# One bank for three running sums: the third product behind the first plain chunk, and a copy by ScalarE in place of an addition

## The chip, the cores and the metric

The kernel runs on 1 core of one Trainium2 chip. The metric is the time of one execution on the device, in microseconds. The engines are called as the profile calls them: PE is TensorE's matmul, PEld its weight load, DVE is VectorE, ACT is ScalarE, POOL is GpSimd, SP is SyncE, which issues the DMAs. `L380` is line 380 of the kernel before.

## The reference, cut to what matters

A decoder trunk of two layers over 256 tokens of width 2048, in float32. Each layer has a mixer (attention and a gated recurrence that share an input and an output projection), a gated FFN, and a small gated embedding, with norms around them. What matters here is that each of these is a set of products `tokens x weights`:

```
proj = h @ w_in                      # 2048 -> all heads
x    = x + norm(mix @ w_out)         # 2048 -> 2048
hid  = silu(h @ w_ffn_gate) * (h @ w_ffn_up)     # 2048 -> 5632, twice
x    = x + norm(hid @ w_ffn_down)    # 5632 -> 2048
g    = gate(x @ w_ple_gate)          # 2048 -> 2048
```

## The kernel before

**Tiles.** The 256 tokens are two blocks of 128 rows. A product is made in columns of 512 (one PSUM bank of 128 x 512 per block), over chunks of 256 rows of the weight matrix. To keep float32's accuracy, weights and activations are each split in a high and a low part. A chunk of weights (tile `wr`, fetched by `fetch_w` L275 on SP) is cast by ACT to its high part `wh` (L281), and DVE subtracts that to get the low part `wl` (L291). One product of a block and a chunk is six matmuls of 128x512: L380 (high x high), L383 (low activations x high weights) and L384 (high activations x low weights), twice each. In the names of the trace, `ck` is a split activation, `sum` (or `nat`) a split sum of activations, `ms` a bank for short use, and `acce`, `acca`, `accc`, `accd` the four accumulators of a pair.

**Pairs.** `paired` works on two columns and both blocks together, 40 times in all (20 for each layer: 2 for w_out, 10 for gate and up, 7 for down, 1 for the embedding's gate). For the first two chunks, `fast` uses a scheme with seven products in place of eight: some products are of sums of tokens (`mix(i)`, made by `mixed`) and of differences of weight chunks (`sub`, L396, in place in the tiles `r11`, `r12`, `r21`, `r22`). The other chunks are plain: `plain` makes one product for each block and chunk.

**The sums in question.** A bank `u` takes the product of block 0 and `r11`; `saved` (L389) has ACT copy it to SBUF as `p1`. Then the product of `mix(2)` is added in the same bank, and ACT copies that as `u2`. A third product, of `mix(3)` and `r12`, has a bank of its own, `u7`. DVE adds `u7` and `u2` to `u3` (L426), and `u3` to `p5` (L427), which is a copy of the first part of `c`. `p1`, `u3`, `u2` and `p5` are added to the accumulators at the end of the pair.

**What sets the order.** The program is written in a plain order, but a scheduler places the instructions on each engine by its own estimates of cost, so the order on an engine is fixed before the run and differs from the text. At run time each engine takes its instructions strictly as they stand, and waits by semaphores. `tick()` lets deferred steps (`later`) in, such as the turning of activations by way of DRAM: `turn<-nat` and `nat<-turn` on SP (L234, L240), with the splits of what comes back by ACT (L179) and DVE (L180). The pools hold 6 tiles `wr`, 7 each of `wh` and `wl`, 12 `nat`, and 4 + 4 PSUM banks (`ms` and `acc`).

Of the kernel before, what the change touches and what calls it, by code (L numbers as in the profile page):

```python
# [12 lines left out]
ALU = mybir.AluOpType  # L13
# [34 lines left out]
def decoder(ctx: ExitStack, tc: tile.TileContext, x, p, positions, w_in, attn_sinks,  # L48
# [16 lines left out]
    V, S, G, T = nc.vector, nc.scalar, nc.gpsimd, nc.tensor  # L65
# [29 lines left out]
    def tick():  # L95
        clock[0] += 1
        for gen in list(running):
            if next(gen, True):
                running.remove(gen)
        for item in [q for q in queue if q[0] <= clock[0]]:  # L100
            queue.remove(item)
            item[1]()

    def nat(shape=(P, W), dt=F32):
        return np_.tile(list(shape), dt, tag="nat", name="nat")

    def bank(shape=(P, W)):
        return pms.tile(list(shape), F32, tag="ms", name="ms")
# [158 lines left out]
    def new_ck():  # L267
        return [xp.tile([P, 4, SEQ], F32R, tag="ck", name="ck", bufs=14) for i in range(2)]
# [4 lines left out]
    def fetch_w(w, c, col):  # L273
        raw = wpr.tile([P, 2, W], F32, tag="wr", name="wr")
        nc.sync.dma_start(raw, w[c * 2 * P:(c + 1) * 2 * P, col:col + W].rearrange(  # L275
            "(k p) n -> p k n", p=P))
        return raw
# [6 lines left out]
    def load_w(w, c, col, raw=None, hi=None):  # L284

        if raw is None:
            raw = fetch_w(w, c, col)
        if hi is None:
            hi = high(raw)
        lo = wps.tile([P, 2, W], F32R, tag="wl", name="wl")  # L290
        marks["lo"] = V.tensor_tensor(lo, raw, hi.bitcast(F32), op=ALU.subtract)  # L291
        return hi, lo
# [68 lines left out]
    def paired(lhs, sums, wa, wb, cols, done_a, done_b, nch=8, row0=0, skews=(0, 0),  # L361
               after=None, mixed_order=False):

        base = row0 // (2 * P)
        opened = {}

        def psum(name):
            return pacc.tile([P, W], F32, tag="acc", name=name)

        def block(c, t):  # L370
            def get(k):
                kt = 2 * c + k
                return tuple(a[:, kt % 4, t * P:(t + 1) * P] for a in lhs[kt // 4])
            return get

        def acc(ps, x, hl):
            hi, lo = hl
            for k in range(2):
                xh, xl = x(k)
                T.matmul(ps, xh, hi[:, k], start=id(ps) not in opened, stop=False,  # L380
                         skip_group_check=True)
                opened[id(ps)] = ps
                T.matmul(ps, xl, hi[:, k], start=False, stop=False, skip_group_check=True)  # L383
                marks["pe"] = T.matmul(ps, xh, lo[:, k], start=False, stop=k == 1,  # L384
                                       skip_group_check=True)

        def saved(ps):
            b = nat()
            S.copy(b, ps)  # L389
            return b  # L390

        def parts(r):
            return load_w(None, 0, 0, raw=r)

        def sub(dst, p, q):
            V.tensor_tensor(dst, p, q, op=ALU.subtract)  # L396

        def fast():
            mix = sums()
            r11, r12 = fetch_w(wa, base, cols[0]), fetch_w(wb, base, cols[1])  # L400
            r21, r22 = fetch_w(wa, base + 1, cols[0]), fetch_w(wb, base + 1, cols[1])
            u = bank()
            acc(u, block(0, 0), parts(r11))
            p1 = saved(u)
            sub(r11, r12, r11)
            c = psum("accc")
            acc(c, mix(1), parts(r11))
            p5 = saved(c)
            tick()
            e = psum("acce")  # L410
            acc(e, block(1, 0), parts(r21))
            sub(r12, r22, r12)
            u7 = bank()
            acc(u7, mix(3), parts(r12))
            tick()
            w22 = parts(r22)
            sub(r22, r22, r11)
            sub(r21, r21, r22)
            acc(u, mix(2), parts(r22))
            u2 = saved(u)  # L420
            a = psum("acca")
            acc(a, block(1, 1), parts(r21))
            tick()
            acc(c, mix(4), w22)
            u3 = nat()
            V.tensor_tensor(u3, u7, u2, op=ALU.add)  # L426
            V.tensor_tensor(p5, u3, p5, op=ALU.add)  # L427
            return e, a, c, (p1, u3), (u2, p5)

        def plain(w, col, banks, skew, end, c0=2, c1=nch):  # L430
            n = c1 - c0
            ws = {}
            for i in range(n + skew):
                if i < n:
                    ws[i] = load_w(w, base + c0 + i, col)
                    acc(banks[0], block(c0 + i, 0), ws[i])
                    if i == n - 1 and end:
                        end(0)
                if i >= skew:
                    acc(banks[1], block(c0 + i - skew, 1), ws[i - skew])  # L440
                tick()
            if end:
                end(1)

        e, a, c, x1, x2 = fast()
        if after:
            after()

        def end_a(t):
            done_a(t, (e, a)[t], x1[t])  # L450

        def end_b(t):
            done_b(t, (c, d)[t], x2[t])
        if mixed_order:
            d = psum("accd")
            plain(wa, cols[0], (e, a), 0, None, c1=nch - 2)
            plain(wb, cols[1], (c, d), 0, None, c1=nch - 2)
            plain(wa, cols[0], (e, a), 0, end_a, c0=nch - 2)
            plain(wb, cols[1], (c, d), 0, end_b, c0=nch - 2)
            return  # L460
        plain(wa, cols[0], (e, a), skews[0], end_a)
        d = psum("accd")
        plain(wb, cols[1], (c, d), skews[1], end_b)

# [203 lines left out]
    for l in range(DEPTH):  # L668
# [4 lines left out]
        mix = {0: attn[0], 1: attn[1]}  # L673
# [450 lines left out]
        for gi, glen in enumerate(FF_GROUPS):  # L1124

            hx = []
            want = ff0 + glen + (glen == 2)
            while len(hidden) < want:
                n = len(hidden)
                gated(n, n == want - 1, hidden[ff0] if n > ff0 else None)  # L1130
            hid = hidden[ff0:ff0 + glen]
            last = gi == len(FF_GROUPS) - 1
            dones = []
            if last:
                nxT = [new_ck() for c in range(4)]
            for s in range(4):
                if gi == 0:
                    macc[s] = sp.tile([P, NT, W], F32, tag="ABCD"[s], name=f"macc{s}")
                if last:
                    gB = load_gain(post_ffn_gain[l], s * W)  # L1140

                def done(t, ps, x, s=s, gB=gB if last else None):
                    m = macc[s][:, t]
                    if gi == 0:
                        V.tensor_tensor(m, ps, x, op=ALU.add)
                        return
                    V.tensor_tensor(m, ps, m, op=ALU.add)
                    if x is not None:
                        V.tensor_tensor(m, x, m, op=ALU.add)
                    if last:  # L1150
                        square_sum(m, ssf[t][:, s:s + 1])
                        V.tensor_tensor(m, m, gB, op=ALU.mult)
                        if s == 3:
                            post_norm(macc, ssf, t, nss, nxT, gain_cols(64, l, 16), (4, 3)[t])
                if last and s == 2:
                    pT2 = sp.tile([P, 2, 2, SEQ], F32R, tag="at", name="pT2")
                    pT = [pT2[:, 0], pT2[:, 1]]
                    for t in range(NT):
                        pn = nat()
                        nc.sync.dma_start(pn[:, 0:256], p[l, 0, t * P:(t + 1) * P, :])  # L1160
                        split_T([pn[:, 0:P], pn[:, P:2 * P]], None, pT, t)
                dones.append(done)
                if last and s >= 2:
                    strip(hid, w_ffn_down[l], s * W, lambda t, ps, done=done: done(t, ps, None),
                          nch=2 * glen, row0=ff0 * W, skew=4 if s == 3 else 0)
                elif s % 2:
                    paired(hid, lambda: hx[0], w_ffn_down[l], w_ffn_down[l], (s * W - W, s * W),
                           dones[s - 1], done, nch=2 * glen, row0=ff0 * W,
                           mixed_order=s == 1)
            ff0 += glen  # L1170
        xT, ss = nxT, nss

# [2 lines left out]
        end = l == DEPTH - 1  # L1175
# [76 lines left out]
```

## Time and profile before

| | us |
|---|---|
| median of 3 runs | 2386.39 |
| lowest, highest | 2385.81, 2387.82 |
| the profiled execution | 2388.4 |
| its span | 2386.7 |

The profiled execution is 2.0 above the median, and 1.7 of its time lies outside its span. Rows of groups read: line, engine, operation, out<-in by names, shapes, count, then busy us, mean ns, and the idle time just before them with what ended it. A matmul of 128x512 is shown with 0.39 us, but the next one starts 0.23 us later: matmuls overlap, and the distance of the starts counts.

### The profile page before, as it was taken

Reading aid. Unit: us, or ns where it says so; the run is one execution under the profiler, and the core shown is the slowest. Engines: PE = TensorE matmul, PEld = TensorE weight load, DVE = VectorE, ACT = ScalarE, POOL = GpSimd, SP = SyncE. Lnnn points to the kernel's source line nnn. Section 1 sums busy time; section 2 is a strip of 40 time slices with the busy share of each in tenths; the row PEclk is TensorE's granted clock in tenths of the full one; section 3 lists DMA queues with packets and bytes.
Section 4 is the critical chain, followed back from the end, with each engine's and each line's share of the span. In section 5 each row is a group of like instructions: output and inputs, shape, how many; then the busy total and the mean of one; then the engine's idle time right before and its main releaser. Section 6 shows DMA issues by size and latency. Waiting matters only on the chain.

```text
span 2386.7 us, 31506 instructions
## 1 busy us (share of the span) xinstructions
PE 2370.5 (99%) x11011; PEld 1963.0 (82%) x11011; DVE 1977.1 (83%) x2611; ACT 1356.6 (57%) x1918; POOL 102.7 (4%) x213
## 2 busy tenths in 40 slices
PE   9999999999999999999999999999999999999999
PEld 7888887887888888888888888878888888888887
DVE  7687987899888888887877879878999978988885
ACT  6565466556555555556656554665555555555563
POOL 3100001000000000001010000010000000000010
PEclk9999999999999999999999999999999999999999
DMA  8666455667566765775776664655766676667753
GB/s 288 217 186 203 150 191 190 219 215 241 188 207 221 234 211 193 248 229 191 244 220 210 182 211 134 230 185 190 225 215 220 206 249 190 214 221 230 246 164 133
DMA packets 299359, 497.64 MB, mean 209 GB/s; under 512 B 23456, under 2 KB 69440, under 8 KB 299200
## 3 DMA queue, kind: packets, MB, share of 16 engines
q1 hardware_dynamic: 298896, 495.54, 64.4%
q8 instruction: 86, 1.41, 0.2%
q14 instruction: 73, 0.60, 0.1%
q10 hardware_dynamic: 240, 0.07, 0.0%
q0 software_dynamic: 64, 0.02, 0.0%
HBM read 470.38 MB, written 25.17 MB: 208 GB/s over the span
## 4 chain that ended last, share of the span: by engine, by line
PE 86%; DVE 8%; DMA 2%; issue 1%; ACT 1%; POOL 1%; SPq 0%; ACTq 0%; DVEq 0%; POOLq 0%
PE acc L307 9%; PE acc L306 9%; PE acc L309 9%; PE accc L384 5%; PE accc L383 5%; PE accc L380 5%; PE acca L380 4%; PE acca L383 4%; PE acca L384 4%; PE acce L380 4%; PE acce L384 4%; PE acce L383 4%; PE accd L380 3%; PE accd L384 3%; PE accd L383 3%; DVE wl L291 3%
## 5 line engine op out<-in xcount | busy, mean ns | idle before, releaser
L281 ACT CAST wh<-wr 128x1024 fp32r<-128x1024 f32 x960 | 995.2, 1053 | 821.8 <-DVE wr L396 239.6
L291 DVE TENSOR_TENSOR wl<-wr,wh 128x1024 fp32r<-128x1024 f32 x960 | 1145.3, 1218 | 265.9 <-ACT wh L281 255.1
L306 PE MATMUL acc<-wh,ck 128*128 128x512 f32 x1056 | 418.1, 396 | 0.3 <-ACT ck L179 0.3
L307 PE MATMUL acc<-wh,ck 128*128 128x512 f32 x1056 | 413.5, 392 | 0.0
L309 PE MATMUL acc<-wl,ck 128*128 128x512 f32 x1056 | 412.4, 392 | 0.8 <-DVE wl L291 0.8
L309 PEld LDWEIGHTS acc<-wl,ck 128*128 128x128 f32 x1056 | 198.8, 188 | 43.2 <-DVE wl L291 1.7
L307 PEld LDWEIGHTS acc<-wh,ck 128*128 128x128 f32 x1056 | 199.0, 188 | 40.2 <-DVE ck L180 0.5
L306 PEld LDWEIGHTS acc<-wh,ck 128*128 128x128 f32 x1056 | 198.8, 188 | 40.4 <-ACT ck L179 0.8
L396 DVE TENSOR_TENSOR wr<-wr 128x1024 f32<-128x1024 f32 x160 | 195.8, 1224 | 6.4 <-DMA wr<-in_w_ffn_down_dram 1.7
L380 PE MATMUL acca<-wh,ck 128*128 128x512 f32 x488 | 190.5, 390 | 1.1 <-ACT wh L281 1.0
L383 PE MATMUL acce<-wh,ck 128*128 128x512 f32 x488 | 190.0, 389 | 0.0
L383 PE MATMUL acca<-wh,ck 128*128 128x512 f32 x488 | 190.0, 389 | 0.0
L384 PE MATMUL acca<-wl,ck 128*128 128x512 f32 x488 | 189.9, 389 | 0.0
L380 PE MATMUL acce<-wh,ck 128*128 128x512 f32 x488 | 189.8, 389 | 0.0
L384 PE MATMUL acce<-wl,ck 128*128 128x512 f32 x488 | 189.8, 389 | 0.0
L380 PE MATMUL accd<-wh,ck 128*128 128x512 f32 x408 | 159.1, 390 | 0.0
L384 PE MATMUL accd<-wl,ck 128*128 128x512 f32 x408 | 158.8, 389 | 0.0
L383 PE MATMUL accd<-wh,ck 128*128 128x512 f32 x408 | 158.7, 389 | 0.0
L380 PE MATMUL accc<-wh,ck 128*128 128x512 f32 x408 | 158.7, 389 | 0.0
L383 PE MATMUL accc<-wh,ck 128*128 128x512 f32 x408 | 158.7, 389 | 0.0
L384 PE MATMUL accc<-wl,ck 128*128 128x512 f32 x408 | 158.7, 389 | 0.0
L380 PEld LDWEIGHTS acca<-wh,ck 128*128 128x128 f32 x488 | 91.6, 188 | 22.3 <-ACT wh L281 3.7
(276 smaller groups left out, 3219.9 us busy)
## 6 DMA issues: line engine op xcount, KB each, us to landing
wr<-in_w_in_dram SPq DMA_DIRECT2D x176, 512.0 KB, 4.9
wr<-in_w_ffn_gate_dram SPq DMA_DIRECT2D x176, 512.0 KB, 4.4
wr<-in_w_ffn_up_dram SPq DMA_DIRECT2D x176, 512.0 KB, 5.9
wr<-in_w_ffn_down_dram SPq DMA_DIRECT2D x176, 512.0 KB, 5.3
wr<-in_w_out_dram SPq DMA_DIRECT2D x64, 512.0 KB, 4.6
wr<-in_w_ple_gate_dram SPq DMA_DIRECT2D x64, 512.0 KB, 5.3
turn<-nat SPq DMA_DIRECT2D x86, 256.0 KB, 2.7
nat<-turn SPq DMA_DIRECT2D x344, 64.0 KB, 3.3
```

Of the source, the lines that this page charges most:

```text
L281: marks["hi"] = S.copy(hi, raw)
L291: marks["lo"] = V.tensor_tensor(lo, raw, hi.bitcast(F32), op=ALU.subtract)
L306: T.matmul(ps[t], xh, hi[:, k], start=first, stop=False)
L307: T.matmul(ps[t], xl, hi[:, k], start=False, stop=False)
L309: marks[t, c] = marks["pe"] = T.matmul(ps[t], xh, lo[:, k], start=False, stop=last)
L380: T.matmul(ps, xh, hi[:, k], start=id(ps) not in opened, stop=False, skip_group_check=True)
L383: T.matmul(ps, xl, hi[:, k], start=False, stop=False, skip_group_check=True)
L384: marks["pe"] = T.matmul(ps, xh, lo[:, k], start=False, stop=k == 1, skip_group_check=True)
L396: V.tensor_tensor(dst, p, q, op=ALU.subtract)
```

## The change

The bank `u7` and the addition L426 go. The third product is put into `u` as well, behind the second, so that `u` itself then holds what was `u3`. This step, now a function `rest`, is called behind the first plain chunk by a new argument `then` of `plain`; ACT copies the bank (`saved`, a third copy of `u`), and DVE adds straight from the bank to `p5`. The product of `mix(4)` is written ahead of that of `acca`, and what the caller passes as `after` comes behind `rest`.

```diff
             sub(r12, r22, r12)
-            u7 = bank()
-            acc(u7, mix(3), parts(r12))
-            tick()
             w22 = parts(r22)
...
             acc(u, mix(2), parts(r22))
             u2 = saved(u)
+            tick()
+            acc(c, mix(4), w22)
             a = psum("acca")
             acc(a, block(1, 1), parts(r21))
             tick()
-            acc(c, mix(4), w22)
-            u3 = nat()
-            V.tensor_tensor(u3, u7, u2, op=ALU.add)
-            V.tensor_tensor(p5, u3, p5, op=ALU.add)
-            return e, a, c, (p1, u3), (u2, p5)
+
+            def rest():
+                acc(u, mix(3), parts(r12))
+                x1.append(saved(u))
+                V.tensor_tensor(p5, u, p5, op=ALU.add)
+            x1 = [p1]
+            return e, a, c, x1, (u2, p5), rest
...
+                if then and i == 0:
+                    then()
                 tick()
...
-        if after:
-            after()
+        def behind_sums():
+            rest()
+            if after:
+                after()
...
-            plain(wa, cols[0], (e, a), 0, None, c1=nch - 2)
+            plain(wa, cols[0], (e, a), 0, None, c1=nch - 2, then=behind_sums)
...
-        plain(wa, cols[0], (e, a), skews[0], end_a)
+        plain(wa, cols[0], (e, a), skews[0], end_a, then=behind_sums)
...
-                           mixed_order=s == 1)
+                           mixed_order=s == 1 and glen > 2)
```

The places of the order below are all in one pair, the first gate/up pair of layer 0 (pair 3 of the 40, counted from 0). The numbers behind names are those of buffers; `ms_4622` before and `ms_4619` after are the bank `u`. First PE, from the second product on, before:

```order
L384 MATMUL ms_4622<-wl_4680,sum_4083 128x512
L380 MATMUL accc_4636<-wh_4672,sum_4083 128x512 [waits Activation_49]
L383 MATMUL accc_4636<-wh_4672,sum_4084 128x512
L384 MATMUL accc_4636<-wl_4674,sum_4083 128x512
L380 MATMUL accc_4636<-wh_4672,sum_4083 128x512
L383 MATMUL accc_4636<-wh_4672,sum_4084 128x512
L384 MATMUL accc_4636<-wl_4674,sum_4083 128x512
L384 MATMUL acca_4690<-wl_4752,ck_3071 128x512
L380 MATMUL acca_4690<-wh_4750,ck_3071 128x512
```

And after:

```order
L384 MATMUL ms_4619<-wl_4666,sum_4081 128x512
L380 MATMUL accc_4633<-wh_4658,sum_4081 128x512 [waits Activation_49]
L383 MATMUL accc_4633<-wh_4658,sum_4082 128x512
L384 MATMUL accc_4633<-wl_4660,sum_4081 128x512
L380 MATMUL accc_4633<-wh_4658,sum_4081 128x512
L383 MATMUL accc_4633<-wh_4658,sum_4082 128x512
L384 MATMUL accc_4633<-wl_4660,sum_4081 128x512
L384 MATMUL acca_4682<-wl_4748,ck_3071 128x512
L380 MATMUL ms_4619<-wh_4711,sum_4081 128x512 [waits Activation_49]
```

The first row is the last matmul of the second product. Seven matmuls later comes, in place of a matmul into `acca`, the first of the third product, in the same bank; it waits for ACT. It is PE's row 2121 of the order and the product's last is row 2126; before, the third product was made at rows 2067 to 2072, far ahead of the second (2111 to 2116), and the second now stands three rows earlier (2108 to 2113).

Second ACT at the same place, before:

```order
L389 COPY nat_4633<-ms_4622 128x512
L389 COPY nat_4647<-accc_4636 128x512
L281 CAST wh_4849<-wr_4847 128x1024 [waits DMAHW4_49,DVE_49,PE_49]
L281 CAST wh_4867<-wr_4865 128x1024 [waits DMAHW5_49,PE_49]
L389 COPY nat_4688<-ms_4622 128x512 [waits PE_49]
```

And after:

```order
L389 COPY nat_4630<-ms_4619 128x512
L389 COPY nat_4644<-accc_4633 128x512
L281 CAST wh_4845<-wr_4843 128x1024 [waits DMAHW4_49,DVE_49,PE_49]
L281 CAST wh_4863<-wr_4861 128x1024 [waits DMAHW5_49,PE_49]
L389 COPY nat_4674<-ms_4619 128x512 [waits PE_49]
L179 CAST ck_4263<-nat_4604 128x4x128 [waits DMAHW6_49,DMAHW7_49,DMAHW1_49,DMAHW0_49]
L389 COPY nat_4721<-ms_4619 128x512 [waits PE_49]
```

The copy of the second sum (`nat_4688`, now `nat_4674`) keeps its place behind two casts that wait for DMAs and for PE; the new copy of the third sum (`nat_4721`) comes two places later.

Third DVE, before:

```order
L291 TENSOR_TENSOR wl_4869<-wr_4865,wh_4867 128x1024 [waits DMAHW5_49,PE_49,Activation_49]
L426 TENSOR_TENSOR nat_4707<-ms_4661,nat_4688 128x512 [waits Activation_49]
L343 TENSOR_TENSOR nat_4808<-ck_3836,ck_3837 128x512
L427 TENSOR_TENSOR nat_4647<-nat_4707,nat_4647 128x512 [waits DVE_49]
L180 TENSOR_TENSOR ck_4266<-nat_4607,ck_4265 128x4x128 [waits DMAHW6_49,DMAHW1_49,DMAHW7_49,DMAHW0_49,Activation_49]
```

And after:

```order
L291 TENSOR_TENSOR wl_4865<-wr_4861,wh_4863 128x1024 [waits DMAHW5_49,PE_49,Activation_49]
L343 TENSOR_TENSOR nat_4804<-ck_3834,ck_3835 128x512
L427 TENSOR_TENSOR nat_4644<-ms_4619,nat_4644 128x512 [waits Activation_49]
L180 TENSOR_TENSOR ck_4264<-nat_4604,ck_4263 128x4x128 [waits DMAHW6_49,DMAHW7_49,DMAHW1_49,DMAHW0_49]
L343 TENSOR_TENSOR nat_4806<-ck_3834,ck_3835 128x512
L291 TENSOR_TENSOR wl_4883<-wr_4879,wh_4881 128x1024 [waits DVE_49,DMAHW2_49,PE_49,Activation_49]
```

L426 is gone; L427 reads the bank and waits for ACT, and the next split of weights on DVE is `wl_4883`, which PE needs first at its row 2189.

More of the change, by code (lines that the diff above doesn't have):

```diff
@@ L423, in fast, with plain @@
             tick()
-            acc(c, mix(4), w22)
-            u3 = nat()
-            V.tensor_tensor(u3, u7, u2, op=ALU.add)
-            V.tensor_tensor(p5, u3, p5, op=ALU.add)
-            return e, a, c, (p1, u3), (u2, p5)
-        def plain(w, col, banks, skew, end, c0=2, c1=nch):
+            def rest():
[4 more added lines that the diff above has]
+            return e, a, c, x1, (u2, p5), rest
+        def plain(w, col, banks, skew, end, c0=2, c1=nch, then=None):
             n = c1 - c0
@@ L443, in plain @@
                 end(1)
-        e, a, c, x1, x2 = fast()
-        if after:
-            after()
+        e, a, c, x1, x2, rest = fast()
+        def behind_sums():
+            rest()
+            if after:
+                after()
         def end_a(t):
```

## The prediction

> **What bounds the kernel now.** I read the page's busy times and clock first, then the groups by shape, then the waits, and last the timeline of ACT and PE around the places that the order changes. The page (busy us, share, instructions; granted clock in tenths, by 40 slices):
>
> ```profile
> PE 2370.5 (99%) x11011; PEld 1963.0 (82%) x11011; DVE 1977.1 (83%) x2611; ACT 1356.6 (57%) x1918; POOL 102.7 (4%) x213
> PEclk9999999999999999999999999999999999999999
> ```
>
> PE is the bound over the whole span and its clock never falls. DVE at 83% and ACT at 57% matter only where PE waits for them. The groups that the change touches, and the two that surround them (count, busy us, mean ns, idle before and what ended it):
>
> ```profile
> L281 ACT CAST wh<-wr 128x1024 fp32r<-128x1024 f32 x960 | 995.2, 1053 | 821.8 <-DVE wr L396 239.6 <-PE acc L307 176.2 <-PE acca L383 121.7
> L389 ACT COPY nat<-ms 128x512 f32<-128x512 f32 x80 | 46.4, 580 | 6.7 <-PE ms L384 6.7
> L427 DVE TENSOR_TENSOR nat<-nat 128x512 f32<-128x512 f32 x40 | 27.4, 686 | 0.4
> L426 DVE TENSOR_TENSOR nat<-ms,nat 128x512 f32<-128x512 f32 x40 | 27.3, 683 | 0.7 <-ACT nat L389 0.4
> ```
>
> What PE and its weight loads wait for in this phase (us in total, times, longest):
>
> ```profile
> PE ms L380 <- ACT wh L281: 1.6, 3, 0.8
> PE acca L380 <- ACT wh L281: 1.0, 4, 0.3
> PEld acca L380 <- ACT wh L281: 3.7, 6, 0.7
> PEld ms L380 <- ACT wh L281: 2.9, 3, 1.2
> PEld ms L380 <- ACT nat L389: 1.3, 4, 0.6
> ```
>
> These are short waits at the change of one pair to the next, for the first casts of the new weights. Counted on PE by starts that come later than one matmul after the one before (0.2275 us, next fence), they lose 5.3 us with their restarts. So a gain has little to come from; a loss needs only a new wait on PE.
>
> **The change, part by part.** The number of products stays, so PE's own work stays. Removed: the addition L426, 40 x 683 ns = 27.3 us of DVE. PE does not wait for it, nor for L427, in any row above, so it is priced at zero; what covers it is PE's backlog of finished weights. Added: 40 copies of the third sum by ScalarE, each like L389's 580 ns, 40 x 0.58 = 23.2 us of ACT, which is idle 43% of the span; no product waits for them, so zero too. L427 now reads PSUM; L426's 683 against L427's 686 ns says that a PSUM operand costs nothing more.
>
> L427 does get a wait: for the third product and, in DVE's order, for the new copy. Behind it on DVE stand the next splits of weights. In the pair whose orders are shown with the change, wl_4883 is the first of them, PE's row 2189, and the third product ends at row 2126: 62 products, 62 x 0.2275 = 14.1 us of cover. At four of the 40 pairs the order leaves 33 to 44 products, at least 7.5 us, enough for the copy, the addition (0.58 + 0.69) and several splits. So zero, and a rival below.
>
> The third part is what I think decides. Before, the third product had its own bank and stood far ahead of the second. Now it goes into the bank of the second, which ScalarE must first have copied. In 22 of 40 pairs (12 gate/up pairs, 8 down pairs, 2 others) the order puts exactly 7 products between the last of the second product and the first of the third: 8 steps x 0.2275 = 1.82 us in which the copy must start and end. On ACT that copy stands behind casts of weights that are needed much later but still on their way from DRAM. The waits of such casts (us, times, longest):
>
> ```profile
> ACT wh L281 <- DMA wr<-in_w_ffn_up_dram: 51.9, 64, 3.5
> ACT wh L281 <- DMA wr<-in_w_ffn_down_dram: 39.8, 36, 3.1
> ```
>
> In the first gate/up pair of layer 0 it looks like this (start us, duration, instruction, idle before): ACT, then PE.
>
> ```profile
> 497.22 1.05 ACT L281 CAST wh<-wr 128x1024 fp32r<-128x1024 f32 x1 [2.17 <-DMA wr<-in_w_ffn_up_dram]
> 498.90 1.05 ACT L281 CAST wh<-wr 128x1024 fp32r<-128x1024 f32 x1 [0.63 <-DMA wr<-in_w_ffn_up_dram]
> 499.86 0.58 ACT L389 COPY nat<-ms 128x512 f32<-128x512 f32 x1
> ```
>
> ```profile
> 498.21 0.39 PE L384 MATMUL ms<-wl,sum 128*128 128x512 f32 x1
> 499.79 0.39 PE L384 MATMUL acca<-wl,ck 128*128 128x512 f32 x1
> 500.02 0.39 PE L380 MATMUL acca<-wh,ck 128*128 128x512 f32 x1
> ```
>
> The second product's last matmul starts at 498.21. The two casts wait for DMA, so the copy runs from 499.86 to 500.44, long after its data are there; nobody minds, as the matmul at 500.02 is another accumulator's. In the changed order the third product stands in that place and could not start before 500.49 (0.05 us from a release to a start, from the k=2 rows below): 0.46 us late. The same reckoning in the last of these pairs:
>
> ```profile
> 2188.07 1.05 ACT L281 CAST wh<-wr 128x1024 fp32r<-128x1024 f32 x1 [3.51 <-DMA wr<-in_w_ffn_up_dram]
> 2189.38 1.06 ACT L281 CAST wh<-wr 128x1024 fp32r<-128x1024 f32 x1 [0.26 <-DMA wr<-in_w_ffn_up_dram]
> 2190.34 0.57 ACT L389 COPY nat<-ms 128x512 f32<-128x512 f32 x1
> ```
>
> ```profile
> 2187.72 0.39 PE L384 MATMUL ms<-wl,sum 128*128 128x512 f32 x1
> 2189.53 0.39 PE L380 MATMUL acca<-wh,ck 128*128 128x512 f32 x1
> ```
>
> 2190.34 + 0.57 + 0.05 - (2187.72 + 1.82) = 1.42 late. Over the 12 gate/up pairs, of which these two are the first and the last, the lateness is 0.46, 0.49, 0.05, none, 0.68, 0.77, 1.23, 1.28, 0.46, 1.08, 0.03, 1.42: 8.0 us. Each wait also costs 0.11 us of restart (below): 11 x 0.11, or 1.3 with the twelfth. Now the second product also comes three matmuls, 0.68 us, earlier in its pair than before, while the casts follow DMAs whose time comes only partly along; so each lateness may grow. Lower end: it grows by nothing, 8.0 + 1.3 = 9.3. Upper end: by the full 0.68, about 12 x 0.68 = 8.1 more, 17.4. I take a third of it, 2.7, since a cast that waits for a DMA waits for one whose buffer the pair itself freed: 9.3 + 2.7 = **+12.0**.
>
> In the down pairs the order of ACT differs: only one cast is left ahead of the copy where two stood before. Pair 18 (ACT, PE):
>
> ```profile
> 1047.87 1.05 ACT L281 CAST wh<-wr 128x1024 fp32r<-128x1024 f32 x1 [3.04 <-DMA wr<-in_w_ffn_down_dram]
> 1049.82 1.05 ACT L281 CAST wh<-wr 128x1024 fp32r<-128x1024 f32 x1 [0.91 <-DMA wr<-in_w_ffn_down_dram]
> 1050.78 0.58 ACT L389 COPY nat<-ms 128x512 f32<-128x512 f32 x1
> ```
>
> ```profile
> 1047.20 0.39 PE L384 MATMUL ms<-wl,nat 128*128 128x512 f32 x1
> 1049.02 0.39 PE L383 MATMUL accc<-wh,ck 128*128 128x512 f32 x1
> ```
>
> Without the second cast the copy starts 0.96 us (1049.82 to 1050.78) after the first one, at 1048.83, ends at 1049.41 and lets the product go at 1049.46, against 1049.02 due: 0.44 late instead of 2.39. One other of these pairs comes out the same, the rest near zero. With the two other pairs and the shift: **+2.0**, between 1 and 5.
>
> The first copy of the bank has a place of the same kind. In the pair ahead (pair 2), ACT, then PE:
>
> ```profile
> 453.13 0.62 ACT L179 CAST ck<-nat 128x512 fp32r<-128x512 f32 x1 [1.70 <-DMA nat<-turn]
> 453.65 1.05 ACT L281 CAST wh<-wr 128x1024 fp32r<-128x1024 f32 x1
> 454.60 0.58 ACT L389 COPY nat<-ms 128x512 f32<-128x512 f32 x1
> ```
>
> ```profile
> 454.71 0.39 PE L380 MATMUL acca<-wh,ck 128*128 128x512 f32 x1
> 455.23 0.50 PE L380 MATMUL ms<-wh,sum 128*128 128x512 f32 x1
> 455.57 0.39 PE L383 MATMUL ms<-wh,sum 128*128 128x512 f32 x1
> ```
>
> The copy ends at 455.18 and PE goes on at 455.23: the 0.05 of above; the next starts 0.34 later instead of 0.2275: the 0.11 of restart. So such a wait is real in this kernel. In the changed order the second product stands nine matmuls, 2.05 us, earlier here, and about as much in the same pair of layer 1 (with 0.7 us in hand there), and three earlier in two others with almost none in hand: 2.05 + 1.35 + 2 x 0.68 = 4.8 if the copy does not move at all. Zero if it comes along, **+2.5** as the middle.
>
> The gate pair of layer 0 had its second copy over 5 us late, behind casts that the new order puts elsewhere: **+0.5**, from 0 to 5.
>
> On the other side the 5.3 us at the changes of pairs: in two pairs the order gives the cast that PE waits for about 1 us more, in two 0.26, elsewhere nothing: **-3.0** with their restarts, between 0 and -5.3.
>
> Sum: 12.0 + 2.0 + 2.5 + 0.5 - 3.0 = +14.0 us. The profiled execution took 2388.4 us (span 2386.7, 1.7 around it), 2.0 over the median of the three runs, and 2402.4 would be its counterpart; for the median 2386.4 + 14.0 = 2400.4.
>
> A rule to weigh here: the Trainium skill, "TensorE: Matmul & The Clock Gate", section "What's actually happening", says that an array idle for a window of about 3.4 us falls to half clock until it has been busy as long again. This trace shows no fall, with waits of at most 0.8 us in PE's rows. By that rule the sum would stay as it is so long as a new wait is below the window; each one above it would add some 1.7 us, an estimate from that page.
>
> **The rivals.**
> (1) The copies are not late. The casts in front of them depend on DMAs, and these on buffers that DVE frees; with 27.3 us less on DVE, or with PE pushed back by the first stall, they could be 0.7 us earlier against the second product. Then from the twelve only 0.53 + 0.58 + 0.38 + 0.72 + 0.07 = 2.3 stays, with 0.5 of restarts, and 2.5 + 0.5 - 3.0 balance: about 2389, no change. For it: the two casts of pair 37 waited 3.51 and 0.26 us, so a little earlier DMA moves all. Against: those weights are requested by SP behind the fetches of transposed blocks, not behind DVE's split.
> (2) Faster: with one addition less per pair, DVE's subtractions L396 end earlier, and ACT's casts, whose largest idle time is put down to just these (239.6 us), too. If they come 0.8 us earlier at every change of pairs, the 5.3 us vanish, and if no third product waits, 2386.4 - 5.3 = 2381.1. It decides only where both hold; the two traced pairs with 1.42 and 0.46 speak against the second.
> (3) DVE stands behind L427 so long that splits come late. It needs a wait above 14.1 us, or 7.5 in the four thin pairs; 1 us in each of these would give 2404. By the Trainium skill, "PSUM — Partial Sum Buffer", section "PSUM bank collisions raise a hardware error", two engines, readers too, must not be in one bank at once. It would put the copy's time ahead of each L427; no row of before shows two readers.
> (4) A wait long enough for the clock to drop, at two places: ten matmuls at half speed are 10 x 0.2275 = 2.3 us more each time, 4.6 on top: 2405. The longest lateness above, 2.39, is not there any more in the new order.
>
> **How the numbers follow.** Forecast 0.68; (1) 0.17; (2) 0.08; (3) 0.04; (4) 0.03. A measurement tells 0.2% apart, 4.8 us. Slower by more than that: 0.68 + 0.04 + 0.03 = 0.75; the same 0.17; faster 0.08. The forecast's own range: 9.3 + 1 + 0 + 0 - 5.3 = +5 at the lower ends, 2391, and 17.4 + 5 + 2.5 + 0.5 - 0 = +25 at the upper ones, 2411. The 8-in-10 range has to take in most of (1): 2387 to 2411. Below it lies (2) and a few hundredths of (1), above it some 0.06.
>
> **What would show it.** Right: in PE's waits a new row, ms matmuls waiting for ACT's copy L389, some 20 times and 8 to 17 us in total, mostly at the start of the third product in gate/up pairs; waits of L281 at pair changes reduced; the added copies near 23 us, DVE 27 us less. Wrong: that row stays below 3 us (then 1 or 2); or PE waits for wl of L291 after L427 (then 3); or a lower PEclk digit (then 4).

## The result, and the profile after

| | us |
|---|---|
| before, median of 5 runs | 2386.39 (2384.49 to 2388.71) |
| changed, median of 5 runs | 2398.61 (2395.88 to 2400.50) |
| ratio, 95% interval | 1.0048, 1.0033 to 1.0063 |
| span of the changed kernel's profiled execution | 2396.9 (before 2386.7) |

The change costs 12.2 us by the medians. The page of the changed kernel (busy us, share, instructions, then the clock row), with its groups for the operations of the change; the addition now reads the bank `ms`:

```profile
PE 2371.4 (99%) x11011; PEld 1959.6 (82%) x11011; DVE 1963.1 (82%) x2571; ACT 1380.1 (58%) x1958; POOL 104.5 (4%) x213
PEclk9999999999999999999999999999999999999999
```

```profile
L389 ACT COPY nat<-ms 128x512 f32<-128x512 f32 x120 | 69.8, 582 | 55.4 <-PE ms L384 55.3
L380 PE MATMUL ms<-wh,sum 128*128 128x512 f32 x104 | 42.6, 410 | 11.8 <-ACT nat L389 11.5 <-ACT wh L281 0.2
L427 DVE TENSOR_TENSOR nat<-ms,nat 128x512 f32<-128x512 f32 x40 | 27.5, 687 | 11.1 <-ACT nat L389 11.1
```

PE has the same 11011 instructions and the same busy time within 1 us, DVE 40 instructions less, ACT 40 more (80 copies of `ms` became 120, 46.4 became 69.8 us). What differs is idle time on PE. Its waits, and those of its weight loads, in the changed kernel:

```profile
PE ms L380 <- ACT nat L389: 11.5, 10, 1.6
PE ms L384 <- DVE wl L291: 0.6, 2, 0.3
PE ms L380 <- ACT wh L281: 0.2, 1, 0.2
PEld ms L380 <- ACT nat L389: 20.8, 28, 2.0
PEld ms L380 <- ACT wh L281: 2.0, 6, 0.6
```

Among PE's own rows the first did not exist before: matmuls into the shared bank wait for ACT's copies, 11.5 us in ten places, up to 1.6 each. All ten are third products of gate/up pairs. The old waits for the casts of a new pair are all but gone (on PE from 1.6 and 1.0 to 0.2); in their place are 0.6 us for DVE's splits.

These are the two pairs that the prediction showed, pair 3 and pair 37, ACT and then PE:

```profile
494.24 1.05 ACT L281 CAST wh<-wr 128x1024 fp32r<-128x1024 f32 x1 [1.69 <-DMA wr<-in_w_ffn_up_dram]
495.86 1.05 ACT L281 CAST wh<-wr 128x1024 fp32r<-128x1024 f32 x1 [0.57 <-DMA wr<-in_w_ffn_up_dram]
496.81 0.58 ACT L389 COPY nat<-ms 128x512 f32<-128x512 f32 x1
...
495.76 0.39 PE L384 MATMUL acca<-wl,ck 128*128 128x512 f32 x1
497.44 0.50 PE L380 MATMUL ms<-wh,sum 128*128 128x512 f32 x1 [1.29 <-ACT nat L389]
497.78 0.39 PE L383 MATMUL ms<-wh,sum 128*128 128x512 f32 x1
...
2198.12 0.58 ACT L389 COPY nat<-ms 128x512 f32<-128x512 f32 x1
...
2197.38 0.39 PE L384 MATMUL acca<-wl,ck 128*128 128x512 f32 x1
2198.75 0.50 PE L380 MATMUL ms<-wh,sum 128*128 128x512 f32 x1 [0.98 <-ACT nat L389]
```

In pair 3 the copy ends at 497.39 and the third product starts at 497.44. It was due 0.2275 us after 495.76: 1.45 late, and 0.11 more for the restart.

Counted by matmuls that start late after the one before them, the places inside `paired` lose 6.8 us before and 19.8 after, 13.0 more. (The 11.5 us of the row are 14.7 in this count: the row counts a wait from the shown end of the matmul before it, 0.16 us after the next one was due, and restarts and the two smallest waits come on top.) The spans differ by 10.2 only, because the profiled execution of the changed kernel was 2.9 us ahead by PE's 301st matmul (68.19 against 71.04), long before the first pair. The medians say 12.2.

### The profile page after: what moved, and what is told of

Same layout as the page of the kernel before. It is cut to its first block, busy times and chain, and to the rows that moved or that the text cites. A ratio compares the mean times of both kernels' runs of the same rounds, so it can differ in the third digit from the quotient of the medians.

```text
span 2396.9 us, 31528 instructions
## 1 busy us (share of the span) xinstructions
PE 2371.4 (99%) x11011; PEld 1959.6 (82%) x11011; DVE 1963.1 (82%) x2571; ACT 1380.1 (58%) x1958; POOL 104.5 (4%) x213
## 4 chain that ended last, share of the span: by engine, by line
PE 86%; DVE 5%; DMA 5%; issue 1%; ACT 1%; SPq 1%; POOL 1%; DVEq 0%; ACTq 0%; POOLq 0%
PE acc L307 9%; PE acc L309 9%; PE acc L306 9%; PE accc L384 5%; PE accc L383 5%; PE accc L380 5%; PE acca L380 4%; PE acca L383 4%; PE acce L384 4%; PE acca L384 4%; PE acce L380 4%; PE acce L383 4%; PE accd L383 3%; PE accd L380 3%; PE accd L384 3%; PE ms L380 2%
## 5 line engine op out<-in xcount | busy, mean ns | idle before, releaser
L281 ACT CAST wh<-wr 128x1024 fp32r<-128x1024 f32 x960 | 997.9, 1055 | 777.6 <-DVE wr L396 195.4
```

Of the source, the lines that this page charges most:

```text
L281: marks["hi"] = S.copy(hi, raw)
```

## The experiments

My theory A: the loss is the third product's wait for the copy of the second sum, and the copy is late because ACT takes it behind two casts whose weights have not come. The rivals: the shared bank, the place of the product or the added copies cost by themselves (B); casts moved back make PE wait elsewhere (C).

| kernel | median us | ratio to before, 95% interval | late starts inside `paired`, us |
|---|---|---|---|
| before | 2386.2 and 2386.6 in the two series | | 6.8 |
| changed | 2398.61 | 1.0048, 1.0033 to 1.0063 | 19.8 |
| copy first, all pairs | 2397.67 | 1.0050, 1.0038 to 1.0063 | 18.3 |
| third product last | 2386.28 | 0.9999, 0.9990 to 1.0008 | 5.0 |
| own bank, no addition | 2381.82 | 0.9984, 0.9975 to 0.9992 | 3.1 |
| before, no addition | 2385.86 | 0.9999, 0.9990 to 1.0008 | 7.2 |
| copy first, 12 pairs | 2385.58 | 0.9995, 0.9986 to 1.0004 | 5.9 |
| copy first, 6 pairs | 2390.84 | 1.0018, 1.0009 to 1.0027 | 10.8 |
| own bank, with addition | 2384.57 | 0.9993, 0.9984 to 1.0002 | 5.8 |

### The copy ahead of the casts, in all pairs

```diff
+                    raw = fetch_w(w, base + c0 + i, col)
+                    with behind("u2") if wa is not wb and w is wb else nullcontext():
+                        hi = high(raw)
-                    ws[i] = load_w(w, base + c0 + i, col)
+                    ws[i] = load_w(w, base + c0 + i, col, raw, hi)
```

`marks["u2"]` is the copy of the second sum.

> The changed kernel, but in the gate/up pairs the casts of the second column's plain chunks may stand on ACT only behind the copy of the second sum. Theory A (the loss is the copy standing behind casts that wait for DMAs): the 14.7 us by which the third products of the 12 gate/up pairs start late in the changed kernel's trace vanish, 2398.6 - 14.7 = about 2384; PE's waits for ACT's copy fall from 11.5 us to below 1. Rival B (the shared bank, the place of the product or the 40 added copies cost time by themselves): those are all still there, so 2396 to 2400. Rival C (the casts, now later, make PE wait for weights instead): A's gain is given back in waits for L281 or L291, 2390 or more.

It took 2397.67 us: by the total, no better than the changed kernel. But the edit did more than the expectation says. `w_ffn_down[l]` makes a new object at each use, so `wa is not wb` held in every pair, and the down pairs, which need the casts soon, had them put back too. Its PE waits:

```profile
PE ms L381 <- ACT wh L281: 4.0, 6, 0.9
PE ms L381 <- ACT nat L390: 1.5, 4, 0.5
PE acce L381 <- ACT wh L281: 1.4, 2, 0.7
PE acca L381 <- ACT wh L281: 1.2, 2, 0.6
PE accc L381 <- ACT wh L281: 0.7, 2, 0.3
```

The waits for the copy (L390 here) fell from 11.5 to 1.5 us, and none of the rest is at one of the 12 places. In their stead PE waits for casts (L281) in and behind the down pairs, 7.3 us in these rows. That is rival C, at other places than I had in mind, and the total alone would have been read as B.

### The copy ahead in the 12 gate/up pairs alone, and in six of them

The same edit with the pairs counted, and the condition `number in (3, 7, 11, 12, 16, 17, 23, 27, 31, 32, 36, 37) and w is wb`. The expectation's word on the pairs 2 and 22 should be on all pairs, as just told.

> The changed kernel with the copy of the second sum ahead of the two casts on ACT in the 12 gate/up pairs alone; the order of ACT is otherwise the same row for row, and in PE's order only the third product moves, one matmul up. (The first experiment of this kind also turned pairs 2 and 22 around, and the order of the down pairs with them, and gave its gain back there.) Theory A: the 14.7 us at the third products go and nothing takes their place: 2398.6 - 14.7 = 2383.9, from 2382 to 2386. Rival B (the shared bank or the added copies cost as such): 2396 to 2400. Rival C (casts behind the copy come late for PE): above 2388, with waits for L281 in the gate/up pairs.

2385.58 us: 13.0 below the changed kernel, where 14.7 were expected. ACT and PE in pair 3 (the copy is L394, the matmuls L385 to L389):

```profile
496.53 0.59 ACT L394 COPY nat<-ms 128x512 f32<-128x512 f32 x1 [2.06 <-PE ms L389]
497.02 1.05 ACT L281 CAST wh<-wr 128x1024 fp32r<-128x1024 f32 x1
498.35 1.05 ACT L281 CAST wh<-wr 128x1024 fp32r<-128x1024 f32 x1 [0.29 <-DMA wr<-in_w_ffn_up_dram]
...
496.11 0.39 PE L389 MATMUL ms<-wl,sum 128*128 128x512 f32 x1
497.47 0.39 PE L389 MATMUL accc<-wl,sum 128*128 128x512 f32 x1
```

The copy now waits only for the second product, its idle time is ended by PE, and it ends at 497.12, before the product in between does. The shared bank, the place of the product (one matmul earlier) and the 120 copies are all still there, so B falls. In this trace none of the 12 third products starts late. Part of what is missing from the full 14.7 us stands in this row:

```profile
PE ms L385 <- ACT wh L281: 1.2, 1, 1.2
```

This is one wait for a cast, at the change to pair 26, which is not one of the 12; and the third product of pair 2 now waits for its copy, 0.6 us with the restart. For the other dose, six pairs:

> As the kernel with the copy ahead in 12 pairs, but only in six of them (3, 11, 16, 23, 31, 36), whose third products start late by 9.0 of the 14.7 us in the changed kernel's trace. Theory A: the gain goes by these places, 2398.6 - 9.0 = 2389.6, from 2387 to 2392, and the other six wait as before. Were the effect one of the whole schedule and not of the places, half the pairs would not bring just their own share.

2390.84 us, 7.8 below the changed kernel. Its row of waits:

```profile
PE ms L385 <- ACT nat L394: 3.9, 6, 1.1
```

The six pairs moved have no wait. The other six still start late by 5.2 us together (5.7 in the changed kernel), though single ones moved by up to 1.1 either way; five of them are in this row, and the sixth wait in it is the third product of pair 22. The loss goes by places, not by the schedule as a whole.

### The third product behind the last plain chunk

```diff
                 if then and i == 0:
                     then()
+                if then and i == n - 1:
+                    rest()
...
-                acc(u, mix(3), parts(r12))
+                with behind("pe"):
+                    acc(u, mix(3), parts(r12))
```

`then` keeps only what the caller passes as `after`.

> The changed kernel, but the third product is issued behind the last plain chunk of the first column in place of the first; ACT's order ahead of the copy of the second sum stays as it is. In the gate/up pairs 43 to 47 matmuls, not 7, then stand between the second and the third product. Theory A: the copy is as late as before, but 8 us or more of other matmuls hide it: about 2384. Rival B (shared bank or added copies as such): 2396 to 2400. Rival D (the bank and the tile of weights are held longer, and something else waits for them): between, with a new wait in PE's rows.

2386.28 us. Here the copy keeps its place behind the two casts. Pair 37, ACT and PE:

```profile
2184.30 1.06 ACT L281 CAST wh<-wr 128x1024 fp32r<-128x1024 f32 x1 [1.10 <-DMA wr<-in_w_ffn_up_dram]
2185.26 0.58 ACT L389 COPY nat<-ms 128x512 f32<-128x512 f32 x1
...
2183.02 0.39 PE L384 MATMUL ms<-wl,sum 128*128 128x512 f32 x1
2184.61 0.39 PE L384 MATMUL acca<-wl,ck 128*128 128x512 f32 x1
2184.83 0.39 PE L380 MATMUL acce<-wh,ck 128*128 128x512 f32 x1
```

The copy ends at 2185.84, a full microsecond after the place where the changed kernel would have put the third product (2184.84). PE goes on with `acce` instead and never stops. So a late copy is harmless if nothing is due. With the experiment before it this closes the case from both sides: moving the copy or moving the product away from it gives the same 12 to 13 us. No new wait of D's kind stands in PE's rows: one wait for a copy of 0.7 us is left, of the second product in the gate pair of layer 0 for the copy of the first sum.

### An own bank at the new place, without the addition

```diff
-                acc(u, mix(3), parts(r12))
-                x1.append(saved(u))
-                V.tensor_tensor(p5, u, p5, op=ALU.add)
+                u7 = bank()
+                acc(u7, mix(3), parts(r12))
+                x1.append(saved(u7))
+                V.tensor_tensor(p5, u7, p5, op=ALU.add)
```

> The changed kernel with the third product in a bank of its own, at the place in the program that the change gives it; ACT copies that bank, DVE adds it to p5. Left out is the addition of the second sum, so the output lacks it; the numbers of ACT copies and of DVE additions are those of the changed kernel. The third product need not wait for any copy. Theory A: no product waits for ACT's copy, about 2384. Rival B (the added copies or the shorter DVE work cost time): 2396 to 2400.

2381.82 us, the fastest of all. ACT's 120 copies are still there, as this group shows:

```profile
L389 ACT COPY nat<-ms 128x512 f32<-128x512 f32 x120 | 67.6, 582 | 43.2 <-PE ms L384 43.2
```

So the added copies cost nothing. (With its own bank the scheduler puts the third product ahead of the second again in the gate/up pairs, so place and bank are undone together there.)

### The addition alone

The kernel before, with `V.tensor_tensor(p5, u7, p5, op=ALU.add)` in place of the two additions, and with `u2` handed on in place of `u3`.

> The kernel before without the addition L426 (the second sum is not added to the third product, which L427 adds to p5 alone; that term is missing from the output). It measures what one addition less per pair, 27.3 us of DVE, is worth by itself. Theory A (PE is the bound, the addition is hidden): 2384 to 2388, the median of before within 2. Rival E (DVE's relief eases the changes of pairs): up to 5.3 us faster, 2381 to 2383; then a part of the -2.9 us seen at pair changes in the changed kernel comes from the addition and not from the new order.

2385.86 us against 2386.17, ratio 0.9999, 0.9990 to 1.0008. DVE's row and two waits of it:

```profile
PE 2368.1 (99%) x11011; PEld 1961.0 (82%) x11011; DVE 1955.0 (82%) x2571; ACT 1357.9 (57%) x1918; POOL 102.6 (4%) x213
PE ms L384 <- DVE wl L291: 2.3, 4, 0.9
PE ms L380 <- ACT nat L389: 0.9, 2, 0.7
```

22 us less on DVE buy nothing that eleven runs can tell: the waits at changes of pairs only took other places (7.2 us in all, 6.8 before). At the eight pairs where the kernel before lost 5.2 us (pairs 5, 6, 9, 14, 25, 26, 29 and 34), 1.5 are left, but six others (2, 10, 15, 22, 30 and 35) lose 4.3 more than they did. So in the old order the removed addition moves these waits and does not take them away. The changed kernel loses 2.5 us at the eight pairs; the next run asks whether the new order does that by itself.

### The kernel before in the new order

```diff
-                acc(u, mix(3), parts(r12))
-                x1.append(saved(u))
-                V.tensor_tensor(p5, u, p5, op=ALU.add)
+                u7 = bank()
+                acc(u7, mix(3), parts(r12))
+                u3 = nat()
+                V.tensor_tensor(u3, u7, u2, op=ALU.add)
+                x1.append(u3)
+                V.tensor_tensor(p5, u3, p5, op=ALU.add)
```

> The changed kernel with the third product in a bank of its own and the old sum by DVE: u3 = u7 + u2 (the addition L426 is back), p5 = u3 + p5, and no third copy by ACT; all results are computed. It is the kernel before in the new order. Theory A: the third product waits for no copy, the addition is hidden, the changes of pairs are eased as in the own-bank run: 2381 to 2384, faster than before by some 0.15%. If the addition back on DVE cost time, it would be above 2386.

2384.57 us, just above the expected 2381 to 2384: 0.9993, 0.9984 to 1.0002, which cannot be told from before. The sure loss of 12 us is gone (here too the third product stands ahead of the second in the gate/up pairs). The easing that was expected is mostly missing:

```profile
PE ms L380 <- ACT wh L281: 1.8, 5, 0.6
```

The run with its own bank and no addition has no such row on PE. At the eight pairs named above this kernel loses 4.3 us, that one 1.8, with nearly the same order on PE. So the new order by itself is not shown to ease the changes of pairs, nor is the removed addition by itself; the traces fit the two together, and no run separates them further. Whether the 2 us are a gain stays open. Of the 2.8 us between the medians of these two runs, which came from two series, 2.7 stand in their late starts (5.8 and 3.1). No version was shown faster than the kernel before with all its results computed.

## Why the prediction was right, point by point

The forecast was 2400.4 in 2387 to 2411; 2398.6 came out, by the mechanism named as decisive.

- *The bound.* PE's row and its matmul count stayed; the loss is idle time on PE. Right.
- *The removed addition at zero.* Measured by itself in the old order: 0.9999. Right there; in the new order the runs with and without it differ by 2.7 us of late starts, so the zero is not shown for it.
- *The added copies at zero.* 120 copies in the run with its own bank and in that with 12 pairs moved, and no loss. Right.
- *L427's wait, covered by 14.1 us.* DVE did wait for the copies, 11.1 us in the group row above; no new PE wait for `wl` is behind it beyond 0.6 us. Right.
- *The 12 gate/up pairs, +12.0.* Measured 14.7 with restarts (pair by pair 1.56, 0.20, 1.48, 0.29, 1.33, 1.58, 1.75, 0.93, 1.00, 1.43, 1.88, 1.25), inside the bounds of 9.3 and 17.4. The sum was a little low: 14.7 - 9.3 = 5.4 of lateness came on top, two thirds of the 8.1 that the second product's 0.68 us could bring, where I took one third. The single pairs do not follow the reckoning: before their restarts they differ from it by -0.5 to +1.7 (0.46 for pair 3 became 1.45, 0.03 for pair 36 became 1.77, 1.42 for pair 37 became 1.14); the casts ahead of the copy wait for single DMAs, in pair 3 to 494.24 and 495.86. So the mechanism and its bounds held, and which pair loses how much was not foreseen. In PE's rows the wait came ten times, not some 20; at the other places the copy came in time or too little late for those rows.
- *The down pairs and two others, +2.0.* About 1.0, nearly all of it restarts of 0.08; only pair 8 waited, 0.25 with its restart. With one cast ahead, the copy comes just in time. Too high. In the two others, pairs 2 and 22, the third product has little in hand: in the run with 12 pairs moved it waited 0.6 us in pair 2, in that with six as long in pair 22.
- *The first copy in four pairs, +2.5.* Nothing: late starts of 0.4 us in all, where these four pairs had lost 0.6 before (0.4 of it in pair 2). I had let the copy come half along; it came along altogether. This is the term most wrongly sized. In pair 2 the split L179, which waited for a DMA until 453.13 before, finds its data at 446.39, and the cast ahead of the copy waits for PE alone. The changed kernel there, ACT and PE:

```profile
446.39 0.62 ACT L179 CAST ck<-nat 128x512 fp32r<-128x512 f32 x1
448.16 1.06 ACT L281 CAST wh<-wr 128x1024 fp32r<-128x1024 f32 x1 [1.15 <-PE acca L383]
449.12 0.57 ACT L389 COPY nat<-ms 128x512 f32<-128x512 f32 x1
...
449.77 0.47 PE L380 MATMUL ms<-wh,sum 128*128 128x512 f32 x1
```

The copy ends at 449.69, the second product starts at 449.77.
- *The gate pair of layer 0, +0.5.* 0.5 there, 0.3 more than before. But 0.4 of it is the second product waiting for the copy of the first sum (0.29 and the restart); the late second copy that the term was about costs 0.08. That the size fits is luck. The trace has this pair at seven products as well, so such pairs are 23, not 22.
- *The changes of pairs, -3.0.* At the eight pairs from 5.2 to 2.5, -2.6, and 0.3 of small stops in the pairs 8 and 18 are gone as well: -2.9. Right in the sum; pairs 6 and 26 got worse, by 0.8 together.
- *The range.* Its upper end takes 2.5 and 0.5 for two terms whose own upper ends the prediction puts at 4.8 and 5. By these it would have been +32, some 2419. It did not come to that.

The measured differences, 14.7 + 1.0 - 0.1 + 0.3 - 2.9 = 13.0, are the 13.0 of late starts inside `paired`. The forecast of 14.0 is this near because 2.7 us too little at the gate/up pairs met 3.8 too much in the down pairs, the first copies and the gate pair: the mechanism was foreseen, the closeness of the total is in part luck. The clock rule of the Trainium skill ("TensorE: Matmul & The Clock Gate", "What's actually happening") changed nothing in the changed kernel: longest wait 1.6 us, PEclk at 9 throughout.

## What to carry to other kernels

An instruction's time is not the price of a merge of two buffers; the new order between a reader and the next writer is. Before a product is put in a bank that another engine has to copy first, look on that engine for what stands ahead of the copy and what that waits for: here 0.58 us of copy stood behind casts that waited for DMAs, and seven matmuls, 1.8 us, were too few to hide it. A late copy is freed in two ways, by taking it ahead of the waiting work or by taking the next writer further away, and the first must be limited to places where the work put back is not itself due.

## What the runs showed of the hardware

The clock fell without any long wait. In the run with the copy first in all pairs, two changes of pairs, one in each layer, have the same matmuls and nearly the same waits. Stretches of that run (us, then busy us and count of PE, PEld, DVE, ACT and POOL, granted clock, DMA share, GB/s):

```profile
550.00:553.00 3.00, 1.49 (x6) 0.93 (x6) 2.96 (x3) 2.73 (x3) 0.00 (x0) 0.97 0.56 173
553.00:556.50 3.50, 3.50 (x11) 2.69 (x10) 3.34 (x4) 3.27 (x5) 0.00 (x0) 0.53 0.80 236
...
1739.50:1742.50 3.00, 1.53 (x6) 0.92 (x6) 2.97 (x3) 2.73 (x3) 0.00 (x0) 1.00 0.53 170
1742.50:1746.00 3.50, 3.50 (x17) 2.86 (x16) 3.50 (x4) 3.50 (x5) 0.00 (x0) 1.00 0.77 224
```

In both, PE did six matmuls in 3 us, with waits of at most 0.93 us. In the first place the clock was then 0.53 for 3.5 us, with 11 matmuls where the twin did 17; the matmuls started 0.43 us apart, in all 1.6 us lost. So the same short waits came ahead of a fall of the clock once, and of none the other time. The Trainium skill ("TensorE: Matmul & The Clock Gate", "What's actually happening") speaks of an activity window that runs freely, which fits such a difference of two like places; what share of idle time it takes, these runs don't show.
